# A samples' list on 128 partitions, and half of each gathered row of the second expert table summed on TensorE during the front

## The chip, the cores and the metric

One core of one Trainium2 chip runs the whole program. The metric is device time in microseconds (us); the time of a kernel is the median of its runs. TensorE is PE, its weight loads PEld, VectorE DVE, ScalarE ACT, GpSimd POOL, SyncE SP. SP and POOL issue DMA transfers: SP the plain loads and stores, POOL the gathers.

## The reference, cut to what matters

One decoder layer for 512 prompt tokens and 8 sample tokens, width 1024. After attention, retention and the output projection comes a mixture of 16384 tiny experts, each one row of `peer_u` and one row of `peer_v` (1024 f32 each, 4 KB). Every token picks 16 experts for each of 8 heads:

```
s = jnp.einsum('thcd,hcnd->thcn', q, sub_keys)   # two axes of 128 keys
sv, si = lax.top_k(s, PEER_TOPK)                 # 16 best of each axis
best, pos = lax.top_k(cand, PEER_TOPK)           # 16 best of their 256 sums
g = jax.nn.softmax(best, -1)
u = peer_u[eid]
a = jax.nn.gelu(jnp.einsum('thkd,td->thk', u, xb))
return jnp.einsum('thk,thkd->td', g * a, peer_v[eid])
```

## The kernel before, in words

The program has a **front** (norm, input projection, attention, retention, output projection `out_proj`, second norm `norm2`, and `product_keys`, the choice of the experts) and behind it a **dense loop**. The 512 prompt tokens go through the front in two waves of 256; the 8 samples ride with them.

The first 256 tokens use **gathered** experts. They form two lists of 128 tokens (one on each partition); the 8 samples form a third list, S, of 64 rows: row 8*h+s is head h of sample s. For every head and every one of its 16 experts a *step* fetches one row for each partition with an indirect DMA on POOL's queue (128 rows of 4 KB, 0.524 MB; for S 64 rows) into one of 8 buffers, and does one DVE instruction on it: a *dot* of a `u` row with the token (L940), or a *sum* `y += w*v` of a `v` row over all 1024 columns (L952 for the first, L954). The dots of head h+1 stand ahead of the sums of head h. The generator `work` yields after each step. There are 512 steps of the two lists and 32 of S, 544 in all.

The other 256 tokens, the second wave, use **all** 128 blocks of 128 experts. Block i loads `ut` (512 KB, on SP's queue, 4 buffers), does 8 matmuls of 256 columns (L1058, below called *a block* or *the a's*; they write `paF` while the front runs, `pa` or a spare `y` bank later) and a gelu; then it loads `vt` (512 KB, 4 buffers), multiplies on DVE by `big` (L1173) and does 4 matmuls of 512 columns into the four `y` banks (L1180, *a y*). `big` holds each token's gate for each expert; `scatter` builds it from the top-k lists of wave two, 8 tokens at a time: three one-hot compares on DVE (`oj` L1148, `oi` L1149, and `oi` times the gates, L1153), matmuls into `pg` (L1159), a copy on ACT (L1161). The 32 scatters of the first 64 blocks stand ahead of the first y.

How many steps of `work` go with which part of the front is set by constants. They are emitted 16 at once when wave two begins, then 7 with each piece of its input projection, 5 with each of 8 pieces of `out_proj`, 3 with each of the 8 heads of `product_keys`; SOON of them with the 32 scatters; and RATE minus all those before are paced over the 128 blocks of the dense loop; what is left is emitted behind the last block. While the front runs, `early` also emits 14 of the first 19 a's. Emission sets the data flow, but a scheduler sets the order on each engine.

In `product_keys` of wave two each head takes two `w_pq` loads (1 MB each, `raw`), 16 projection matmuls each of 264 columns (L157), scores (`psco`, L846), and top-k on DVE (from `MAX8`, L258, on); the samples' scores gather in `pss`. Behind the last head the samples' scores are turned (`psr`, L860) and S gets its own top-k (`gS` at L358, `eidS` at L351). Then the gates of wave two are turned (L1116) and the first scatter can begin.

Of the kernel before, what the change touches and what calls it, by code (L numbers as in the profile page):

```python
# [9 lines left out]
F32 = mybir.dt.float32  # L10
F32R = mybir.dt.float32r
BF16 = mybir.dt.bfloat16
I32 = mybir.dt.int32
U32 = mybir.dt.uint32
AF = mybir.ActivationFunctionType
OP = mybir.AluOpType
# [15 lines left out]
GT = 256  # L32
# [11 lines left out]
NG = DT // 8  # L44
STEPS = (16, 7, 5, 3)
BLOCKS = 2
SOON, RATE = 24, 590
AHEAD0 = 14
# [3 lines left out]
def step_kernel(ctx, tc, x_prompt, x_sample, cache_k, cache_v, state_ret, norm1_g, w_in, ret_gn_g,  # L52
# [135 lines left out]

    selb = consts.tile([8, 64], F32, name="selb")
    selT = consts.tile([64, 8], F32, name="selT")  # L190
    iota16 = consts.tile([128, TOPK], BF16, name="iota16")
# [9 lines left out]
    def tables():  # L201
# [28 lines left out]
        nc.vector.tensor_scalar(gnb, gnb, 0.5, None, op0=OP.mult)  # L230
        ii = su.tile([8, 8, 8], I32, name="ii")
        nc.gpsimd.iota(ii, pattern=[[0, 8], [1, 8]], base=0, channel_multiplier=-1)
        nc.vector.tensor_scalar(selb, ii.rearrange("p a b -> p (a b)"), 0.0, None, op0=OP.is_equal)
        pst = ps_tile("tr", "pst")
        nc.tensor.transpose(pst[:64, :8], selb, ident[:8, :8])
        nc.vector.tensor_copy(selT, pst[:64, :8])

# [356 lines left out]
    def samples_attention():  # L594
# [69 lines left out]
        pw = ps_tile("x", "pw")  # L664
        nc.tensor.matmul(pw[:64, :8], selb, snew, start=True, stop=True)
        lnew = sp.tile([64, 1], F32, name="lnew")
# [26 lines left out]
        pw8 = ps_tile("x", "pw8")  # L693
        nc.tensor.matmul(pw8[:8, :8], selT, hsel, start=True, stop=True)
        a8 = sp.tile([8, 512], F32, name="a8", tag="s8")
# [66 lines left out]
    def out_proj(pool, c2, x, xs, ssq):  # L762

        for c, pas in project(w_out2, [c2], range(8)):
            n = WT + (8 if xs is not None else 0)
            cs = slice(c * 128, (c + 1) * 128)
            oT = pool.tile([128, WT + 8], F32, name="oT", bufs=2)
            nc.scalar.activation(oT[:, :n], pas[0][:, :n], AF.Copy)
            pn = ps_tile("tr", "pno")
            for b in range(2):  # L770
                nc.tensor.transpose(pn[:, b * 128:(b + 1) * 128], oT[:, b * 128:(b + 1) * 128], ident)
            nc.vector.tensor_tensor(out=x[:, :, cs], in0=blk(pn[:, :WT]), in1=x[:, :, cs], op=OP.add)
            sq = pool.tile([128, 128], F32, name="osq", bufs=2)
            for b in range(2):
                nc.scalar.activation(sq, x[:, b, cs], AF.Square, accum_out=ssq[:, b, c:c + 1])
            if xs is not None:
                pn2 = ps_tile("x", "pn2o")
                nc.tensor.transpose(pn2[:8, :128], oT[:, WT:], ident)
                nc.vector.tensor_tensor(out=xs[:, cs], in0=pn2[:8, :128], in1=xs[:, cs], op=OP.add)
                nc.scalar.activation(sq[:8], xs[:, cs], AF.Square, accum_out=ssq[:8, 2, c:c + 1])  # L780
            yield

    def norm2(pool, w, x, xs, ssq, hn):
# [24 lines left out]
        if xs is not None:  # L808
            pS = ps_tile("x", "pt2s")
            for k in range(KB):  # L810
# [13 lines left out]
    def product_keys(w, lists, listS, hn):  # L824
# [3 lines left out]
        if w:  # L828
            pss = ps_tile("x", "pss")
        for d in lists:  # L830
# [24 lines left out]
        if w:  # L855
# [63 lines left out]
    def gather(tab, d, h, k, name):  # L919
# [4 lines left out]
        return t  # L924

    def experts(d, rows, hr):
        p, H = d["p"], d["H"]
        y = pe.tile([128, D], F32, name="y", tag="y")[:p]
# [6 lines left out]
        def dots(h):  # L935
            a = pe.tile([128, TOPK], F32, name="a", tag="a", bufs=3)[:p]
            for k in range(TOPK):
                yield
# [3 lines left out]
            w = pe.tile([128, TOPK], F32, name="gw", tag="gw", bufs=3)[:p]  # L942
            nc.scalar.activation(w, a, AF.Gelu_apprx_tanh)
            nc.vector.tensor_tensor(out=w, in0=w, in1=d["g"][:p, h, :], op=OP.mult)
            return w

        def sums(h, w):
            for k in range(TOPK):
                yield
                v = gather(v_tab, d, h, k, "v")  # L950
                if h == 0 and k == 0:
                    nc.vector.tensor_scalar(y, v[:p], w[:, 0:1], None, op0=OP.mult)  # L952
# [39 lines left out]
    def gathered():  # L992
# [3 lines left out]
        store = finish((y[:, 0:512], y[:, 512:]), y, 128, x, yp2[128:GT, :])  # L996
        y64, x = yield from delayed(experts(listS, [hnr[GT:, :]] * 8, slice(512, 520)), 12, store)
        yS = gp.tile([128, D], F32, name="yS", tag="rows")[:8]
# [26 lines left out]
    def run(g, n=1):  # L1025
        for _ in range(n):
            if g is not None:
                next(g, None)

    pools["ap"] = inB.enter_context(tc.tile_pool(name="apB", bufs=2, side="right"))  # L1030

# [266 lines left out]
```

## Time and profile before

| | before |
|---|---|
| median of 3 runs | 1723.51 us (1723.35 to 1728.24) |
| the profiled execution | 1735.22 us, span 1733.3 us |
| PE busy | 1525.3 us, 88% |
| DVE busy | 1209.2 us, 70% |
| ACT busy | 414.0 us, 24% |
| POOL busy | 786.7 us, 45% |
| moved by DMA | 506.88 MB, mean 292 GB/s |
| chain that ended last | PE 65%, DVE 17%, DMA 10%, issue 4% |

The profiled execution is 11.7 us longer than the median of the runs. Its stages, in us from the span's start: wave two's input projection and mixer to about 536 (with gathers from 366 on), `out_proj` and `norm2` to about 598, `product_keys` and the a's to 770, the 32 scatters to 857, the dense loop to about 1635, and the end of it with the samples' list to 1733.

### The profile page before, as it was taken

The page shows a single profiled execution, that of the slowest core. Times are in us where ns is not written, and L with a number is a line of the kernel's source. Part 1 is how long each engine was busy: PE and PEld are TensorE (multiplying, and loading weights), DVE is VectorE, ACT ScalarE, POOL GpSimd, SP SyncE. Part 2 cuts the span into 40 slices and gives each one's busy share as a digit, 9 for nine tenths or more (in the row PEclk, how much of TensorE's full clock was granted, in tenths as well). Part 3 has the DMA queues.
Part 4 walks back from the last instruction along what each step waited for, and adds up shares of the span by engine and source line. Part 5 has one row for each costly group of instructions (what it writes and reads, how often), then busy time and mean ns, then how long its engine had stood idle before and what let it go on. Part 6 is the DMA issues. An engine that isn't in the chain of part 4 may idle for free.

```text
span 1733.3 us, 21787 instructions
## 1 busy us (share of the span) xinstructions
PE 1525.3 (88%) x7544; PEld 1115.3 (64%) x7544; DVE 1209.2 (70%) x2893; ACT 414.0 (24%) x846; POOL 786.7 (45%) x672
## 2 busy tenths in 40 slices
PE   5987679997763698895799999999999999999986
PEld 4976537876652587785566766666766666666632
DVE  5766614688998689999997666666556555555665
ACT  5743623342121211245411121111111000000001
POOL 2155230045567565318366444444445544544551
PEclk9998899998886799995599999999999999999999
DMA  6576574479999899764599999999998999999996
GB/s 195 156 215 206 194 221 129 116 244 349 329 357 355 325 354 355 248 209 143 170 372 388 386 367 327 332 345 350 344 348 315 386 356 368 356 365 363 319 256 182
DMA packets 213326, 506.88 MB, mean 292 GB/s; under 512 B 16424, under 2 KB 103000, under 8 KB 213088
## 3 DMA queue, kind: packets, MB, share of 16 engines
q0 software_dynamic: 82208, 295.80, 47.6%
q1 hardware_dynamic: 131008, 209.68, 36.2%
q8 instruction: 60, 0.98, 0.2%
q14 instruction: 50, 0.41, 0.1%
HBM read 495.56 MB, written 9.86 MB: 292 GB/s over the span
## 4 chain that ended last, share of the span: by engine, by line
PE 65%; DVE 17%; DMA 10%; issue 4%; ACT 1%; POOL 1%; SPq 0%; DVEq 0%; POOLq 0%; ACTq 0%
PE y L1180 23%; PE pa L1058 22%; PE pa L157 8%; DVE u L940 3%; DVE y L954 3%; DMA vt<-in_peer_v 3%; PE pg L1159 3%; DVE oi L1153 2%; DMA raw<-in_w_out 2%; PE paF L1058 1%; DMA raw<-in_w_pq 1%; DVE oj L1148 1%; DMA pq<-sq_d 1%; PE psc L438 1%; PE pa L127 1%
## 5 line engine op out<-in xcount | busy, mean ns | idle before, releaser
L922 POOL DMA_INDIRECT u<-in_peer_u,eidL x256 | 337.6, 1319 | 369.2 <-PE pT L452 113.3
L1180 PE MATMUL y<-vt,ge 128*128 128x512 f32 x1024 | 464.0, 598 | 6.9 <-DMA vt<-in_peer_v 6.7
L922 POOL DMA_INDIRECT v<-in_peer_v,eidL x256 | 322.3, 1259 | 317.9 <-DVE y L954 125.0
L1058 PE MATMUL pa<-hnD,ut 128*128 128x256 f32 x1792 | 407.5, 381 | 0.5 <-ACT ge L1062 0.5
L1058 PEld LDWEIGHTS pa<-hnD,ut 128*128 128x128 f32 x1792 | 338.8, 191 | 76.9 <-issue 35.4
L954 DVE SCALAR_TENSOR_TENSOR y<-v,gw,y 128x1024 f32<-128x1024 f32 (+1 forms) x269 | 346.2, 1287 | 19.5 <-DMA v<-in_peer_v,eidS 12.1
L940 DVE CUSTOM_DVE_ANT_0 u<-u,hq 128x1024 f32<-128x1024 f32 (+1 forms) x272 | 324.2, 1217 | 30.4 <-DMA u<-in_peer_u,eidL 21.0
L1180 PEld LDWEIGHTS y<-vt,ge 128*128 128x128 f32 x1024 | 195.1, 192 | 212.6 <-issue 203.2
L1173 DVE TENSOR_TENSOR ge<-ge,big 128x256 f32<-128x256 f32 x128 | 51.4, 421 | 199.0 <-ACT ge L1062 186.7
L1062 ACT ACTIVATE ge<-pa 128x256 f32<-128x256 f32 x112 | 43.0, 384 | 503.1 <-PE pa L1058 411.9
L157 PE MATMUL pa<-hnD,raw 128*128 128x256 f32 (+1 forms) x512 | 125.1, 398 | 12.1 <-DMA raw<-in_w_pq 12.1
L1159 PEld LDWEIGHTS <-oj 128*128 128x128 bf16 x1536 | 101.0, 167 | 53.3 <-DVE oi L1153 35.1
L157 PEld LDWEIGHTS pa<-hnD,raw 128*128 128x128 f32 x512 | 99.6, 199 | 35.0 <-DMA raw<-in_w_pq 12.9
L157 PE MATMUL pa<-xTB,raw 128*128 128x256 f32 x448 | 105.1, 387 | 2.4 <-ACT pr L547 1.5
L1148 DVE TENSOR_TENSOR oj<-iota,l 128x1024 bf16<-128x1024 bf16 x64 | 44.0, 689 | 74.8 <-PE pg L1159 71.4
L157 PEld LDWEIGHTS pa<-xTB,raw 128*128 128x128 f32 x448 | 84.8, 195 | 14.6 <-ACT pr L547 1.9
L1159 PE MATMUL pg<-oi,oj 128*128 128x64 bf16 x1152 | 76.8, 231 | 15.0 <-DVE oi L1153 14.4
L1161 ACT ACTIVATE big<-pg 128x512 f32<-128x512 f32 x48 | 53.6, 1116 | 145.0 <-PE pg L1159 125.3
L126 PE MATMUL pa<-xT,wh 128*128 128x264 f32 x224 | 70.7, 316 | 8.6 <-ACT xT L119 4.6
L127 PE MATMUL pa<-xT,wh 128*128 128x264 f32 x224 | 68.7, 307 | 0.1
L128 PE MATMUL pa<-xT,wl 128*128 128x264 f32 x224 | 67.7, 302 | 0.6 <-DVE wl L120 0.6
L1153 DVE TENSOR_TENSOR oi<-oi,lx 128x1536 bf16<-128x1536 bf16 x64 | 60.4, 949 | 0.0
(515 smaller groups left out, 1742.9 us busy)
## 6 DMA issues: line engine op xcount, KB each, us to landing
ut<-in_u_turned SPq DMA_DIRECT2D x128, 512.0 KB
vt<-in_peer_v SPq DMA_DIRECT2D x128, 512.0 KB
raw<-in_w_in SPq DMA_DIRECT2D x56, 512.0 KB
raw<-in_w_pq SPq DMA_DIRECT2D x16, 1024.0 KB
raw<-in_w_out SPq DMA_DIRECT2D x8, 1024.0 KB
kv<-in_cache_k_win POOLq DMA_DIRECT2D x24, 256.0 KB
kv<-in_cache_v_win POOLq DMA_DIRECT2D x24, 256.0 KB
u<-in_peer_u,eidL POOLq DMA_INDIRECT x256
```

The lines of the kernel that those rows point to most:

```text
L126: nc.tensor.matmul(out, wh, xh, start=first, stop=False)
L127: nc.tensor.matmul(out, wh, xl, start=False, stop=False)
L128: nc.tensor.matmul(out, wl, xh, start=False, stop=last)
L157: nc.tensor.matmul(pa[:, :n], part[:, k, :], x[0][:, k, :], start=(k == 0), stop=(k == KB - 1))
L922: nc.gpsimd.indirect_dma_start(out=t[:p], out_offset=None, in_=tab, in_offset=bass.IndirectOffsetOnAxis(ap=d["eid"][:p, h, k:k + 1], axis=0))
L940: nc.vector.tensor_tensor_reduce(out=u[:p], in0=u[:p], in1=hn, scale=1.0, scalar=0.0, op0=OP.mult, op1=OP.add, accum_out=a[:, k:k + 1])
L954: nc.vector.scalar_tensor_tensor(y, v[:p], w[:, k:k + 1], y, op0=OP.mult, op1=OP.add)
L1058: nc.tensor.matmul(pa, ut[:, k, :], hnD[:, k, :DT], start=(k == 0), stop=(k == KB - 1))
L1148: nc.vector.tensor_tensor(out=oj, in0=iota128, in1=lJ[:, None, ts].to_broadcast([128, 128, 8]), op=OP.is_equal)
L1153: marks[c] = nc.vector.tensor_tensor(out=oi3, in0=oi[:, None].to_broadcast([128, 3, ne, 64]), in1=lx[:, 1:, None].to_broadcast([128, 3, ne ...
L1159: nc.tensor.matmul(pg_[:, t * ni:(t + 1) * ni], oj[:, :, t], oi3[:, z, :, es], start=(z == 0), stop=(z == 2))
L1180: nc.tensor.matmul(yps[b][q], ge[:, b * 128:(b + 1) * 128], vt[:, q * 512:(q + 1) * 512], start=(i == 0), stop=(i == NKEY - 1))
```

## The change

Part one: S is kept in a second form, `wideS`, on 128 partitions: partition 64*q + 8*h + s holds experts 8*q to 8*q+7 of head h of sample s. So it takes 8 gathers of 128 rows for the dots and 8 for the sums, in place of 16 and 16 of 64 rows. Four small SP transfers (`gW` <- `gS`, `eidW` <- `eidS`, 64x8 each) make it; they stand behind S's top-k. `selb`/`selT`, which sum S's rows for each sample, become 128 wide, and `hq` is loaded in 16 pieces of 8 rows.

Part two: until the front ends, a sum is split. ACT makes `dg` = identity times the weights of the 128 tokens (128x128), PE adds `dg` times the left 512 columns of `v` to a PSUM bank `vsum`, and DVE adds the right 512 columns alone. There are 64 such matmuls (L964 of the new file), and one with a zero `dg` that ends the accumulation; then DVE copies the bank into the left half of `y`. `vsum` holds the PSUM bank "x", so three small users of that bank move to others.

Part three: constants. With 2 in place of 3 steps for each head of `product_keys`, SOON 16 for 24 and RATE 574 for 590, the steps paced over the dense loop stay 402 (590-164-24 and 574-156-16).

```
-STEPS = (16, 7, 5, 3)
+STEPS = (16, 7, 5, 2)
-SOON, RATE = 24, 590
+SOON, RATE = 16, 574
...
-    selb = consts.tile([8, 64], F32, name="selb")
-    selT = consts.tile([64, 8], F32, name="selT")
+    selb = consts.tile([8, 128], F32, name="selb")
+    selT = consts.tile([128, 8], F32, name="selT")
...
-                pn2 = ps_tile("x", "pn2o")
+                pn2 = ps_tile("s", "pn2o")
...
-            pS = ps_tile("x", "pt2s")
+            pS = ps_tile("s", "pt2s")
...
-            pss = ps_tile("x", "pss")
+            pss = ps_tile("o", "pss")
...
             lockstep([tk_finish(qp, listS, 0, 1)])
+            for q in range(2):
+                for nm in ("eid", "g"):
+                    nc.sync.dma_start(wideS[nm][q * 64:(q + 1) * 64, 0, :],
+                                      listS[nm][:64, 0, q * TOPK // 2:(q + 1) * TOPK // 2])
...
+    wideS = {"p": 128, "H": 1, "K": TOPK // 2, "g": pD.tile([128, 1, TOPK // 2], F32, name="gW"),
+             "eid": pD.tile([128, 1, TOPK // 2], I32, name="eidW")}
...
-                if h == 0 and k == 0:
+                if "bank" in half:
+
+                    dg = pe.tile([128, 128], F32, name="dg", tag="dg", bufs=2)
+                    nc.scalar.activation(dg, ident, AF.Copy, scale=w[:, k:k + 1])
+                    nc.tensor.matmul(half["bank"], dg, v[:, :512], start=(h == 0 and k == 0), stop=False)
+                    half["y"] = y
+                    if h == 0 and k == 0:
+                        nc.vector.tensor_scalar(y[:, 512:], v[:p, 512:], w[:, 0:1], None, op0=OP.mult)
+                    else:
+                        nc.vector.scalar_tensor_tensor(y[:, 512:], v[:p, 512:], w[:, k:k + 1], y[:, 512:],
+                                                       op0=OP.mult, op1=OP.add)
+                elif h == 0 and k == 0:
                     nc.vector.tensor_scalar(y, v[:p], w[:, 0:1], None, op0=OP.mult)
                 else:
                     nc.vector.scalar_tensor_tensor(y, v[:p], w[:, k:k + 1], y, op0=OP.mult, op1=OP.add)
...
-        y64, x = yield from delayed(experts(listS, [hnr[GT:, :]] * 8, slice(512, 520)), 12, store)
+        y64, x = yield from delayed(experts(wideS, [hnr[GT:, :]] * 16, slice(512, 520)), 12, store)
...
+    half["bank"] = ps_tile("x", "vsum")
...
     EARLY = step[0]
+
+    dg = pe.tile([128, 128], F32, name="dg", tag="dg", bufs=2)
+    nc.vector.memset(dg, 0.0)
+    nc.tensor.matmul(half["bank"], dg, keysT[:, 0:4, :].rearrange("p a b -> p (a b)"), start=False, stop=True)
+    nc.vector.tensor_copy(half["y"][:, :512], half.pop("bank"))
     front.close()
```

How the change moves the steps, counted in DVE's order: the steps (dots + sums) that stand ahead of five marks.

| mark on DVE | before | after |
|---|---|---|
| last `yo` (L479), end of the mixer | 48 + 30 = 78 | 48 + 21 = 69 |
| `xo` of `norm2` (L797) | 64 + 43 = 107 | 62 + 32 = 94 |
| second `oi` of the scatters (L1153) | 96 + 67 = 163 | 92 + 64 = 156 |
| 32nd of them | 106 + 80 = 186 | 96 + 74 = 170 |
| last `ge` times `big` (L1173) | 502 of 544 | 486 of 528 |

Behind the last mark 42 steps are left in both: 10 sums of list two and 32 of S before, 26 sums and 16 of the wide list after.

On PE, in `product_keys`, at the projections (L157) and scores (L841, L846) of the late heads. Before:

```order
L841 MATMUL pss<-qT,keysT 128x8
L846 MATMUL psco<-keysT,qT 128x128 x3
L157 MATMUL pa<-hnD,raw 128x264 x16
L841 MATMUL pss<-qT,keysT 128x8
L846 MATMUL psco<-keysT,qT 128x128
```

and of the change, at about the same place (L964 is the new matmul, L1079 the a's, which were L1058):

```order
L846 MATMUL psco<-keysT,qT 128x128 x3
L157 MATMUL pa<-hnD,raw 128x264 x3
L964 MATMUL vsum<-v,dg 128x512
L157 MATMUL pa<-hnD,raw 128x264 x2
L964 MATMUL vsum<-v,dg 128x512
L157 MATMUL pa<-hnD,raw 128x264 x3
L841 MATMUL pss<-qT,keysT 128x8
L846 MATMUL psco<-keysT,qT 128x128
L157 MATMUL pa<-hnD,raw 128x264 x3
L964 MATMUL vsum<-v,dg 128x512
L1079 MATMUL paF<-hnD,ut 128x256 x2
L964 MATMUL vsum<-v,dg 128x512
```

The projections of one head, in one piece before, are now cut by `vsum` matmuls, each of which needs its gathered `v` row and its `dg`. Of the 64, 16 stand ahead of `out_proj`, 16 between there and the end of `norm2`, and 32 behind, ahead of the last head's scores.

On PE at the end of `product_keys`, from the last scores to the a's that stand ahead of the first scatter. Before:

```order
L846 MATMUL psco<-keysT,qT 128x128
L1058 MATMUL paF<-hnD,ut 128x256 x8
L841 MATMUL pss<-qT,keysT 128x8
L846 MATMUL psco<-keysT,qT 128x128 x3
L1058 MATMUL paF<-hnD,ut 128x256 x16
L860 MATMUL psr<-ident,sst 64x128 x2
L1058 MATMUL paF<-hnD,ut 128x256 x48
```

and of the change:

```order
L1079 MATMUL paF<-hnD,ut 128x256 x6
L841 MATMUL pss<-qT,keysT 128x8
L846 MATMUL psco<-keysT,qT 128x128 x3
L1079 MATMUL paF<-hnD,ut 128x256 x7
L1115 MATMUL vsum<-keysT,dg 128x512
L860 MATMUL psr<-ident,sst 64x128 x2
L1079 MATMUL pa_6482<-hnD,ut 128x256 x8
```

Before, 8 of the 14 early a's stand behind the last scores, and 9 further a's behind those, ahead of the first `pg`. Now 7 matmuls of one early a stand behind them, and the same 9 further a's: 7.1 blocks have moved ahead of the last scores.

On DVE among the scatters (`oj`, `oi` and the product L1153, now L1174, L1175, L1179; L954 and L974 are sums). Before:

```order
L1149 TENSOR_TENSOR oi<-iotaE,lx 128x512
L1148 TENSOR_TENSOR oj<-iota_6315,l_6319 128x1024
L1153 TENSOR_TENSOR oi_6716<-oi,lx 128x1536
L954 SCALAR_TENSOR_TENSOR y<-v,gw,y 128x1024
L1153 TENSOR_TENSOR oi_6752<-oi,lx 128x1536
L1149 TENSOR_TENSOR oi<-iotaE,lx 128x512
L954 SCALAR_TENSOR_TENSOR y<-v,gw,y 128x1024
L1148 TENSOR_TENSOR oj<-iota_6315,l_6319 128x1024
L1153 TENSOR_TENSOR oi_6788<-oi,lx 128x1536
```

and of the change:

```order
L1174 TENSOR_TENSOR oj<-iota_6491,l_6495 128x1024
L1179 TENSOR_TENSOR oi_6922<-oi,lx 128x1536
L974 SCALAR_TENSOR_TENSOR y<-v,gw,y 128x1024
L1175 TENSOR_TENSOR oi<-iotaE,lx 128x512
L1174 TENSOR_TENSOR oj<-iota_6491,l_6495 128x1024
L1175 TENSOR_TENSOR oi<-iotaE,lx 128x512
L1174 TENSOR_TENSOR oj<-iota_6491,l_6495 128x1024
L1179 TENSOR_TENSOR oi_6958<-oi,lx 128x1536
L1179 TENSOR_TENSOR oi_6997<-oi,lx 128x1536
```

Between the second and the 32nd scatter there were 10 dots and 13 sums; now there are 4 dots and 10 sums.

## Rows read from the trace of the kernel before

**Rows 1.** Windows by stage: engines' busy us, TensorE's granted clock, DMA share, GB/s.

```profile
core 0: us, PE busy (x) PEld busy (x) DVE busy (x) ACT busy (x) POOL busy (x), PEclk, DMA share, GB/s
366.00:536.00 170.00, 117.90 (x571) 96.50 (x571) 151.53 (x454) 38.18 (x74) 105.49 (x85) 0.85 0.97 339
536.00:598.00 62.00, 33.66 (x128) 25.16 (x127) 40.85 (x69) 16.61 (x63) 38.22 (x30) 0.75 0.94 343
598.00:634.00 36.00, 35.64 (x168) 31.04 (x169) 29.89 (x69) 6.67 (x14) 28.47 (x21) 0.88 0.97 358
634.00:701.00 67.00, 62.01 (x303) 53.20 (x303) 66.65 (x261) 13.23 (x32) 34.07 (x31) 0.97 0.96 343
701.00:728.00 27.00, 21.42 (x100) 18.16 (x99) 27.00 (x128) 7.09 (x15) 10.03 (x8) 0.96 0.89 310
728.00:770.00 42.00, 41.38 (x184) 35.64 (x184) 40.90 (x209) 13.40 (x33) 0.24 (x1) 0.94 0.48 155
770.00:857.00 87.00, 53.97 (x794) 50.55 (x793) 86.57 (x134) 45.74 (x63) 48.41 (x25) 0.56 0.54 168
857.00:1635.00 778.00, 778.00 (x3281) 527.68 (x3282) 487.39 (x697) 93.73 (x182) 394.24 (x315) 1.00 0.95 354
1635.00:1733.00 98.00, 79.75 (x173) 32.01 (x171) 65.18 (x90) 11.20 (x22) 35.90 (x35) 0.93 0.87 229
```

**Rows 2.** What PE waited for, 366 to 598: us, times, longest.

```profile
PE py L482 <- DVE yo L479: 34.9, 4, 13.0
PE pa L157 <- DMA raw<-in_w_out: 14.5, 2, 12.6
```

**Rows 3.** What PE waited for, 598 to 701.

```profile
PE pa L157 <- DMA raw<-in_w_pq: 4.9, 2, 3.4
PE pt L804 <- DVE xo L797: 3.6, 1, 3.6
```

**Rows 4.** The chain, dense loop: start, us; x counts matmuls and weight loads.

```profile
892.19 3.45 PE pa L1058 x16
895.64 3.43 PE y L1180 x8
```

**Rows 5.** DVE's timeline: `norm2`, the last head's MAX8, and the first scatters.

```profile
start us, us, engine line op out<-in xcount [idle before <-releaser]
597.56 0.75 DVE L797 TENSOR_SCALAR xo<-xo,rr__5168 128x1024 f32<-128x1024 f32 x1
...
711.12 0.84 DVE L258 MAX8 valL<-sc 128x8 f32<-128x128 f32 x4
...
767.47 1.82 DVE L1153 TENSOR_TENSOR oi<-oi,lx 128x1536 bf16<-128x1536 bf16 x2
```

**Rows 6.** PE's timeline: the last head's scores and what follows.

```profile
700.29 0.92 PE L846 MATMUL psco<-keysT,qT 128*128 128x128 f32 x6
701.04 7.07 PE L1058 MATMUL paF<-hnD,ut 128*128 128x256 f32 x32
```

**Rows 7.** One line's instructions (ns min/median/max): a DVE sum of 512 columns, a 128x128 ACT.

```profile
L1260 DVE SCALAR_TENSOR_TENSOR xb<-xb,rr__11992,gfb x4: 742/743/750, 1727.3 to 1729.3; 128x512 f32<-128x512 f32 x4
...
L775 ACT ACTIVATE osq<-xo x16: 292/294/311, 548.9 to 586.4; 128x128 f32<-128x128 f32 x16
```

**Rows 8.** Where S's gates `gS` end on DVE: ns, start.

```profile
L358 DVE TENSOR_TENSOR gS<-gS,tsm x1: 163/163/163, 750.3 to 750.3; 64x16 f32<-64x16 f32 x1
```

**Rows 9.** DVE by line, 770 to 857: sums and dots among the scatters.

```profile
L954 DVE SCALAR_TENSOR_TENSOR y<-v,gw,y 128x1024 f32<-128x1024 f32 x13 | 16.6, 1278 | 0.0
L940 DVE CUSTOM_DVE_ANT_0 u<-u,hq 128x1024 f32<-128x1024 f32 x13 | 15.7, 1212 | 0.0
```

**Rows 10.** DMA in the dense loop, 1336 to 1635.

```profile
DMA packets 29445, 107.38 MB, mean 359 GB/s; under 512 B 3263, under 2 KB 3263, under 8 KB 29431
```

**Rows 11.** DMA at the end, 1636 to 1714, with the issues of this stretch.

```profile
DMA packets 5845, 20.38 MB, mean 261 GB/s; under 512 B 878, under 2 KB 878, under 8 KB 5842
...
vt<-in_peer_v SPq DMA_DIRECT2D x17, 512.0 KB
...
u<-in_peer_u,eidS POOLq DMA_INDIRECT x16
v<-in_peer_v,eidS POOLq DMA_INDIRECT x16
```

**Rows 12.** DVE by line, 1635 to 1716: the samples' steps, on 64 rows.

```profile
L940 DVE CUSTOM_DVE_ANT_0 u<-u,hq 64x1024 f32<-64x1024 f32 x16 | 19.4, 1215 | 9.3 <-DMA u<-in_peer_u,eidS 9.3
L954 DVE SCALAR_TENSOR_TENSOR y<-v,gw,y 64x1024 f32<-64x1024 f32 x15 | 19.2, 1280 | 12.2 <-DMA v<-in_peer_v,eidS 12.1
```

**Rows 13.** PE's timeline at the end: L1001 sums the samples' rows.

```profile
1712.53 3.67 PE L1180 MATMUL y<-vt,ge 128*128 128x512 f32 x8 [0.39 <-DMA vt<-in_peer_v]
1716.13 1.88 PE L1001 MATMUL pa<-y,selT 64*8 64x512 f32 x4
1717.94 3.70 PE L1180 MATMUL y<-vt,ge 128*128 128x512 f32 x8
```

More of the change, by code (lines that the diff above doesn't have):

```diff
@@ L230, in tables @@
         nc.vector.tensor_scalar(gnb, gnb, 0.5, None, op0=OP.mult)
-        ii = su.tile([8, 8, 8], I32, name="ii")
-        nc.gpsimd.iota(ii, pattern=[[0, 8], [1, 8]], base=0, channel_multiplier=-1)
+        ii = su.tile([8, 16, 8], I32, name="ii")
+        nc.gpsimd.iota(ii, pattern=[[0, 16], [1, 8]], base=0, channel_multiplier=-1)
         nc.vector.tensor_scalar(selb, ii.rearrange("p a b -> p (a b)"), 0.0, None, op0=OP.is_equal)
         pst = ps_tile("tr", "pst")
-        nc.tensor.transpose(pst[:64, :8], selb, ident[:8, :8])
-        nc.vector.tensor_copy(selT, pst[:64, :8])
+        nc.tensor.transpose(pst[:, :8], selb, ident[:8, :8])
+        nc.vector.tensor_copy(selT, pst[:, :8])
     def tk_new(pool, name, p, heads, eid):
@@ L664, in samples_attention @@
         pw = ps_tile("x", "pw")
-        nc.tensor.matmul(pw[:64, :8], selb, snew, start=True, stop=True)
+        nc.tensor.matmul(pw[:64, :8], selb[:, :64], snew, start=True, stop=True)
         lnew = sp.tile([64, 1], F32, name="lnew")
@@ L693, in samples_attention @@
         pw8 = ps_tile("x", "pw8")
-        nc.tensor.matmul(pw8[:8, :8], selT, hsel, start=True, stop=True)
+        nc.tensor.matmul(pw8[:8, :8], selT[:64], hsel, start=True, stop=True)
         a8 = sp.tile([8, 512], F32, name="a8", tag="s8")
@@ L924, in gather @@
         return t
+    half = {}
     def experts(d, rows, hr):
-        p, H = d["p"], d["H"]
+        p, H, K = d["p"], d["H"], d.get("K", TOPK)
         y = pe.tile([128, D], F32, name="y", tag="y")[:p]
@@ L936, in dots @@
             a = pe.tile([128, TOPK], F32, name="a", tag="a", bufs=3)[:p]
-            for k in range(TOPK):
+            for k in range(K):
                 yield
@@ L942, in dots @@
             w = pe.tile([128, TOPK], F32, name="gw", tag="gw", bufs=3)[:p]
-            nc.scalar.activation(w, a, AF.Gelu_apprx_tanh)
-            nc.vector.tensor_tensor(out=w, in0=w, in1=d["g"][:p, h, :], op=OP.mult)
+            nc.scalar.activation(w[:, :K], a[:, :K], AF.Gelu_apprx_tanh)
+            nc.vector.tensor_tensor(out=w[:, :K], in0=w[:, :K], in1=d["g"][:p, h, :], op=OP.mult)
             return w
         def sums(h, w):
-            for k in range(TOPK):
+            for k in range(K):
                 yield
                 v = gather(v_tab, d, h, k, "v")
-                if h == 0 and k == 0:
+                if "bank" in half:
[9 more added lines that the diff above has]
+                elif h == 0 and k == 0:
                     nc.vector.tensor_scalar(y, v[:p], w[:, 0:1], None, op0=OP.mult)
```

## The prediction

> **What bounds the kernel now.** I read the windows by stage first [rows 1]. From 366 to 598 DMA is at 0.97 and 0.94 of its time while PE is busy for 152 of 232 us and DVE for 192: the gathers and the weights set the pace, and PE's waits there are for `yo`, which stands on DVE behind steps, and for weight loads [rows 2]. From 598 to 701 three things are near their limit together: PE 97.7 of 103 us, DVE 66.65 of the last 67, DMA 0.96 to 0.97. From 701 to 770 PE has 62.8 of 69 us, DVE 67.9, and DMA falls to 0.48. Among the scatters DVE is busy for 86.57 of 87 us and PE waits for it. In the dense loop PE is busy for all of 778 us. At the end PE, DVE and DMA all have gaps. So a gain counts in full only where its own resource is the limit: gathers up to 598, PE or DVE up to 770, DVE to 857, PE after that.
>
> A number for "no change": about 0.3%, 5.2 us of 1723.5, is what a measurement of this kernel tells from nothing. The terms below are differences in the profiled execution's own time (1735.22 us, span 1733.3); I take them over to the median, 11.7 us lower, unscaled, since 0.7% of terms of 50 us is nothing.
>
> **The change, part by part.** *Prices.* A gather is 0.524 MB, at the 339 GB/s of [rows 1] 1.54 us of DMA. A `vsum` matmul has the shape of a y's (128x128 by 512 columns): 3.43 us for four in the chain, 0.857 us each; an a is 3.45 us [rows 4]. 32 of the new matmuls are 27.4 us. A sum of 512 columns on DVE is 0.743 us by the same operation of that size [rows 7], against 1.278 of a whole one [rows 9]: 0.535 less. A `dg` on ACT is no more than the 0.3 us of a 128x128 activation [rows 7], and ACT is busy for a fifth of its time there; nothing, unless a matmul waits for its `dg`.
>
> *(1) Up to `norm2`.* By DVE's order 94 steps stand ahead of `norm2`'s `xo` and not 107: 13 gathers fewer, 13 x 1.54 = 20 us if DMA sets the whole stretch, nothing if another does. In this stretch 32 `vsum` matmuls come to PE (27.4 us), which has 80 us free, and DVE is relieved of 17 us besides the 13 steps. DMA's share is 0.94 to 0.97, so I take most of it: **-18** (0 to -20). The half sums by themselves buy nothing here, as neither PE nor DVE is the limit; the shift of steps does.
>
> *(2) From `norm2` to the last scores.* Before, 597.56 [rows 5] to 701.04 [rows 6], 103.5 us. PE gets 32 `vsum` matmuls, 27.4 us, and 7.1 a's that stood behind the scores, 24.5 us: 51.9 more. PE's waits of 8.5 us [rows 3] can take some of it. Bounds +43 and +52, and +35 should a `vsum` cost less than a y's matmul; taken **+45**. DMA agrees: 62 gathers instead of some 30 before the last scores (156 - 94, since every `vsum` stands ahead of them), 15 loads of 1 MB and ten of 0.5 MB are 53 MB, less about 2 MB already under way, at 350 GB/s 146 us, beside the 148.5 of this sum.
>
> *(3) From the last scores to the second `oi`.* Before, 701.04 to 769.3 (767.47 + 1.82) [rows 5], 68.2 us: 10.1 until the last head's MAX8, as DVE was late, then 58.2 with 3 sums and 227 other rows of DVE's order; without the sums (3.8 us) 0.24 us a row. Now 181 rows stand there and no step: 43.3 us. DVE's lateness shrinks too: from `norm2` to that MAX8 its steps are 30 dots and 32 half sums, 60 us, where 32 dots and 21 sums were 66; with 46 rows moved ahead (11 us) it has 119 us of work in 148. I take 4.7 us of delay, 48 in all: **-20.2** (-15 with the old delay, -21). Hidden under it: PE's nine a's (31 us) and the loads `gW`. Those stand on SP's queue ahead of the last two of the nine `ut`, and wait for `gS`; `gS` came 19 us before 769.3 [rows 8], and two a's need 6.9 of it. If the loads take more than 12 us, the first `pg` waits for them. So the scatters begin at -18 + 45 - 20.2 = +6.8.
>
> *(4) The scatters.* DVE sets them. 6 dots and 3 sums fewer stand among them: 6 x 1.212 + 3 x 1.278 [rows 9] = **-11.1** (-9, should DVE wait now and then for PE).
>
> *(5) The dense loop.* PE has no idle time, its work is the same, and 316 steps of whole gathers lie in it in both (186 to 502, 170 to 486): **0**. Were PE to have gaps there, DVE with 487 us of 778 and DMA with 0.95 say that DMA would come next.
>
> *(6) The end.* 42 steps are left behind the last gate product in both, but the 32 on 64 rows were 8.4 MB, and with 10 whole ones 13.6; now 42 whole ones are 22.0 MB. The stretch moved 20.4 MB in 78 us, 261 GB/s [rows 11]; with 8.4 more at the loop's 359 [rows 10] it is 28.8 MB in 80.2 us, +2. DVE's instructions there are as many and as long (1.215 and 1.280 us on 64 rows [rows 12], 1.212 and 1.278 on 128). PE's order has the samples' selector two y's before its end instead of one [rows 13], 3.4 us more if PE waited for the samples; the y just before waited for `vt` and the selector began 0.0 us behind it, so I take none. **+2** (0 to +10).
>
> The 261 GB/s are with 64-row gathers in flight, the 359 with whole ones; the row shows the two rates, not the reason, and DVE waited 21 us for the half gathers. The Trainium skill's page "SBUF — State Buffer" (section "Door 1: The DMA port swizzle (why `[64,N]` ≈ `[32,N]`)") says that partitions 0 to 63 reach 8 of the 16 ports of the memory, so that a transfer to them alone has half the bandwidth. The rates agree with it in kind. By its figure for a large transfer to all 128 partitions, 328 GB/s, the 28.8 MB would be an estimated 88 us, +10 in place of +2.
>
> Sum: -18 + 45 - 20.2 - 11.1 + 0 + 2 = -2.3 us: 1723.5 - 2.3 = **1721**.
>
> **The rivals.**
> *A, the gain of the first stretch stays (faster).* PE's 52 us between `norm2` and the scores shrink: a `vsum` at the 0.592 us that the trace models for a y's matmul instead of 0.857 takes 8.5 off, and the end at nothing 2 more: about -12, 1711. For it: PE has its weights' load beside the matmul. Against: the y's of the same shape never went faster than 0.857 on end.
>
> *B, PE waits for rows (slower).* A `vsum` needs its gathered row, and PE runs in order, so behind a late `v` wait projections, the retention of wave two and then `yo`. In [rows 2] PE never waited for a gather; now it can 64 times, where DMA is at 0.97. If (1) is lost whole, the sum is -2.3 + 18 = +16, 1739. It decides from 8 us lost on. Against: DVE waited for the same rows already, and `yo` stood behind them.
>
> *C, the end keeps its rate (slower).* At 261 GB/s the 28.8 MB are 110 us, +32 instead of +2: 1751. For it: `vt` and gathers share the engines there, and PE waits for `vt`. Against: whole gathers with `vt` and `ut` ran at 359 for 300 us before. By the rule of the Trainium skill named above the half rows were the cause, which would speak against C.
>
> *D, the loads of `gW` block SP (slower).* If the two `ut` behind them come late, first scatter and all after it are later: 10 us, 1731. Against: 12 us of slack in (3).
>
> **How the numbers follow.** The forecast within 5 us of 1721 has 0.37; A 0.34; B 0.15; C 0.06; D 0.08. The forecast lies within 0.3%, except for a small part of it at the lower edge, which about balances what of A falls within; A is faster; B, C and D are slower, though B and D partly occur at sizes that can't be told from none. Faster 0.37, same 0.37, slower 0.26. The range reaches from a full A with the low bound of the end's price (1706) to a full B (1739); it leaves out C and part of the others. The likeliest case's own range is 1716 to 1726.
>
> **What would show it.** (1) `xo` of `norm2` some 18 us earlier, with DMA still above 0.93 ahead of it; PE's waits for `yo` smaller. (2) the last scores 27 us later than 701, PE without idle time since `norm2`. (3) the second `oi` 48 us behind them, at about 776. (4) 76 us of scatters instead of 87. (5) the loop with PE at 100%. (6) the end with over 330 GB/s, and DVE's waits for S's rows gone or short. Wrong it is if PE's list of waits names `v` rows with over 8 us (B), if the stretch behind the loop is over 105 us (C), if the a's ahead of the first `pg` wait for `ut` (D), or if the last scores come by 717 (A).

## The result, and the profile after

The changed kernel is slower: 1739.58 us, median of 7 runs (1733.98 to 1744.4), against 1728.24 for the kernel before beside it (7 runs, 1723.35 to 1732.03). The ratio is 1.0072, 95% interval 1.0047 to 1.0097: some 12 us. Forecast were 1721 and no measurable change.

The profiled execution took 1741.94 us, span 1740.2. The windows by stage of the changed kernel, in the cuts of [rows 1]:

```profile
core 0: us, PE busy (x) PEld busy (x) DVE busy (x) ACT busy (x) POOL busy (x), PEclk, DMA share, GB/s
366.00:536.00 170.00, 145.72 (x671) 112.54 (x670) 136.42 (x455) 50.90 (x106) 99.29 (x81) 0.92 0.96 338
536.00:598.00 62.00, 40.63 (x155) 29.22 (x155) 37.90 (x74) 19.58 (x73) 36.75 (x27) 0.78 0.85 313
598.00:634.00 36.00, 36.00 (x154) 27.18 (x153) 18.32 (x66) 8.49 (x21) 14.68 (x15) 1.00 0.81 271
634.00:701.00 67.00, 61.24 (x256) 46.49 (x254) 56.77 (x251) 16.34 (x39) 35.29 (x32) 0.95 0.94 343
701.00:728.00 27.00, 26.61 (x127) 22.77 (x128) 23.94 (x91) 7.29 (x14) 13.54 (x11) 1.00 0.88 340
728.00:770.00 42.00, 40.41 (x193) 34.81 (x191) 31.29 (x200) 11.95 (x24) 0.00 (x0) 1.00 0.35 108
770.00:857.00 87.00, 55.59 (x773) 52.34 (x772) 84.60 (x156) 47.00 (x73) 39.82 (x16) 0.61 0.43 136
857.00:1635.00 778.00, 776.27 (x3320) 527.51 (x3319) 487.92 (x716) 96.72 (x186) 391.12 (x315) 1.00 0.95 354
```

Read the columns of PE and DVE between 598 and 728. Before, PE was full from 598 to 634 (35.64 of 36 us) and DVE from 634 to 728 (66.65 of 67 and 27.00 of 27). Now PE is full in the first window and in the third (26.61 of 27), and DVE in none: it is busy for 18 of 36 us in the first. DMA, which had 0.96 to 0.97 from 598 to 701, has fallen to 0.81 in the first window: its loads and gathers wait for buffers that PE holds (SP's queue waits 25.4 us for PE there, against 10.2 before; POOL's gathers 8.4 us for `vsum` matmuls).

The marks of the stages, from the timelines of DVE and PE of the changed kernel (they answer to [rows 5, 6]); DVE's `MAX8` of the last head now waits 10.13 us for the scores:

```profile
582.94 0.75 DVE L797 TENSOR_SCALAR xo<-xo,rr__5348 128x1024 f32<-128x1024 f32 x1
```

```profile
739.02 0.91 PE L846 MATMUL psco<-keysT,qT 128*128 128x128 f32 x6
739.78 3.19 PE L1079 MATMUL paF<-hnD,ut 128*128 128x256 f32 x14
...
860.97 8.60 PE L1206 MATMUL y<-vt,ge 128*128 128x512 f32 x16 [1.73 <-DVE ge L1199]
```

```profile
740.61 0.87 DVE L258 MAX8 valL<-sc 128x8 f32<-128x128 f32 x4 [10.13 <-ACT sc L850]
...
782.10 1.82 DVE L1179 TENSOR_TENSOR oi<-oi,lx 128x1536 bf16<-128x1536 bf16 x2
```

`norm2` comes 14.6 us sooner than before, the last scores 39 us later, the second `oi` 14.6 later, the first y 4.2 later. One profile is one execution, and executions differ by some 10 us; so both kernels were profiled a second time (below). The table has, for each profile, the first gathered dot, the stages from mark to mark (first dot, `xo` of `norm2`, start of the last of the last head's scores, end of the second `oi`, start of the first y, start of the last gate product, end of the span), all in us, to about 0.1.

| kernel | first dot at | to `norm2` | to the last scores | to the second `oi` | to the first y | loop | end |
|---|---|---|---|---|---|---|---|
| before | 369.7 | 227.9 | 103.3 | 68.4 | 87.5 | 778.9 | 97.7 |
| before, again | 371.2 | 221.4 | 101.4 | 66.9 | 87.0 | 778.6 | 97.1 |
| the change | 371.1 | 211.8 | 156.8 | 44.2 | 77.1 | 780.6 | 98.6 |
| the change, again | 362.3 | 210.2 | 157.8 | 44.2 | 76.7 | 781.1 | 98.3 |
| list and constants alone | 370.3 | 223.8 | 112.2 | 52.3 | 84.4 | 778.8 | 95.4 |
| half sums alone | 369.3 | 211.7 | 153.6 | 43.6 | 88.1 | 778.5 | 101.8 |
| half sums end ahead of `out_proj` | 373.4 | 201.6 | 115.4 | 67.2 | 75.7 | 780.6 | 98.2 |
| 7 early a's | 366.3 | 217.0 | 129.5 | 43.7 | 85.8 | 779.4 | 94.8 |
| narrow matmuls | 371.7 | 196.8 | 118.4 | 57.0 | 83.4 | 776.3 | 97.8 |
| 7 early a's, no half sums | 369.8 | 222.2 | 101.3 | 53.9 | 87.7 | 779.2 | 94.7 |
| 48 half sums, 10 early a's | 365.4 | 208.8 | 120.7 | 67.2 | 78.2 | 779.6 | 95.7 |
| 4 early a's | 365.6 | 214.3 | 120.4 | 54.1 | 90.3 | 781.3 | 99.3 |
| end ahead of `out_proj`, 7 early a's | 371.2 | 211.7 | 96.3 | 83.8 | 79.1 | 777.2 | 98.7 |

The means of two profiles each give change minus before: -13.7, +55.0, -23.5, -10.4, +2.1, +1.1, in all +10.6 us, against the 12 of the timed runs. The loss lies in one stage, that from `norm2` to the last scores; the stages ahead of it and behind it win most of it back.

### The profile page after: what moved, and what is told of

Its sections match the earlier page's. It is cut to its first block, busy times and chain, and to the rows that moved or that the text cites. A ratio compares the mean times of both kernels' runs of the same rounds, so it can differ in the third digit from the quotient of the medians.

```text
span 1740.2 us, 22103 instructions
## 1 busy us (share of the span) xinstructions
PE 1568.5 (90%) x7674; PEld 1133.5 (65%) x7674; DVE 1158.3 (67%) x2871; ACT 437.2 (25%) x908; POOL 763.9 (44%) x656
## 5 line engine op out<-in xcount | busy, mean ns | idle before, releaser
L929 POOL DMA_INDIRECT u<-in_peer_u,eidL x256 | 329.0, 1285 | 395.7 <-PE pT L452 114.4
L1079 PE MATMUL pa<-hnD,ut 128*128 128x256 f32 x1792 | 407.7, 381 | 1.6 <-issue 1.6
L1079 PEld LDWEIGHTS pa<-hnD,ut 128*128 128x128 f32 x1792 | 338.6, 191 | 77.7 <-issue 36.8
L949 DVE CUSTOM_DVE_ANT_0 u<-u,hq 128x1024 f32<-128x1024 f32 x264 | 315.4, 1221 | 19.9 <-DMA u<-in_peer_u,eidL 19.2
L974 DVE SCALAR_TENSOR_TENSOR y<-v,gw,y 128x1024 f32<-128x1024 f32 x198 | 253.7, 1281 | 22.2 <-DMA v<-in_peer_v,eidL 11.7
L157 PE MATMUL pa<-hnD,raw 128*128 128x256 f32 (+1 forms) x512 | 127.6, 396 | 0.3 <-DMA raw<-in_w_pq 0.3
L157 PEld LDWEIGHTS pa<-hnD,raw 128*128 128x128 f32 x512 | 99.4, 198 | 29.9 <-issue 14.2
L157 PE MATMUL pa<-xTB,raw 128*128 128x256 f32 x448 | 109.0, 394 | 4.5 <-DMA raw<-in_w_in 4.5
L157 PEld LDWEIGHTS pa<-xTB,raw 128*128 128x128 f32 x448 | 86.5, 198 | 21.9 <-issue 8.1
L1174 DVE TENSOR_TENSOR oj<-iota,l 128x1024 bf16<-128x1024 bf16 x64 | 44.0, 688 | 82.6 <-PE pg L1185 75.2
L964 PE MATMUL vsum<-v,dg 128*128 128x512 f32 x128 | 65.8, 610 | 5.9 <-DMA v<-in_peer_v,eidL 5.0
```

Of the source, the lines that this page charges most:

```text
L157: nc.tensor.matmul(pa[:, :n], part[:, k, :], x[0][:, k, :], start=(k == 0), stop=(k == KB - 1))
L929: nc.gpsimd.indirect_dma_start(out=t[:p], out_offset=None, in_=tab, in_offset=bass.IndirectOffsetOnAxis(ap=d["eid"][:p, h, k:k + 1], axis=0))
L949: nc.vector.tensor_tensor_reduce(out=u[:p], in0=u[:p], in1=hn, scale=1.0, scalar=0.0, op0=OP.mult, op1=OP.add, accum_out=a[:, k:k + 1])
L964: nc.tensor.matmul(half["bank"], dg, v[:, :512], start=(h == 0 and k == 0), stop=False)
L974: nc.vector.scalar_tensor_tensor(y, v[:p], w[:, k:k + 1], y, op0=OP.mult, op1=OP.add)
L1079: nc.tensor.matmul(pa, ut[:, k, :], hnD[:, k, :DT], start=(k == 0), stop=(k == KB - 1))
```

## The experiments

Theory 1, formed on these windows: the half sums' matmuls and the a's that now stand among them cost their full time on PE in `product_keys`, because PE had nothing free there; the late scores delay all that follows. Rivals: theory 2, PE's waits for gathered rows in its order, with the slower clock behind one; theory 3, the samples' list or the constants.

**Both kernels once more.**

> The kernel before, unchanged, profiled once more: which of its stages vary from one execution to the next. Its first profile was of an execution of 1735.2 us, above all its seven timed runs (1723.4 to 1732.0). Expected: the first y at 850 to 857 us, the last gate product 778 to 779 us behind it, and the difference to the first profile in the stages ahead of 770 that wait for DMA.

1725.48 us, span 1723.6. The last gate product came 778.6 us behind the first y, as expected; the first y itself came at 847.9, 2 us ahead of the expected 850 to 857. Of the 9.7 us that this execution is shorter than the first, 6.5 lie between the first dot and `norm2`, where DMA is at 0.97 and 0.94 of its time [rows 1], and 1.9 and 1.5 in the two stages behind.

> The changed kernel, unchanged, profiled once more, for what varies between two executions. Expected: from norm2's end to the last scores 152 to 158 us again (157 in its first profile, 101 and 103 in the two of before), the second oi 43 to 46 us behind them, the first y 77 us behind that.

1732.36 us, span 1730.6. The stages from `norm2` on agree with the first profile within about 1 us each; of the 9.6 us between the two executions 8.8 were there at the first dot already (371.1 and 362.3). So the +55 us is no accident of one execution.

**The parts apart.** The list and the constants without the half sums, then the half sums without these:

```
-                if "bank" in half:
...
-                elif h == 0 and k == 0:
+                if h == 0 and k == 0:
```

> The samples' list on 128 partitions and the new constants, without the half sums (each sum is again one DVE instruction of 1024 columns). In its order 155 steps stand ahead of the second oi instead of 163, and 15 among the scatters instead of 23; up to norm2 the order is that of before. Theory 1 (the half sums cost: 32 more matmuls and 7 a's ahead of the last scores on a PE that is full there): none of that is here, so 8 steps less ahead of the scatters and 8 less among them give some -8 to -18 us against before, ratio 0.990 to 0.996. Theory 3 (the loss lies in the samples' list or the constants): +5 us or more, ratio over 1.003.

Ratio 0.9949 (0.9927 to 0.9970), 1718.53 us: faster than before, as theory 1 has it. Theory 3 falls.

```
-STEPS = (16, 7, 5, 2)
+STEPS = (16, 7, 5, 3)
-SOON, RATE = 16, 574
+SOON, RATE = 24, 590
...
-        y64, x = yield from delayed(experts(wideS, [hnr[GT:, :]] * 16, slice(512, 520)), 12, store)
+        y64, x = yield from delayed(experts(listS, [hnr[GT:, :]] * 8, slice(512, 520)), 12, store)
```

> The half sums alone, with the samples' list on 64 partitions and the constants of before (3 steps a head, 24 among the scatters, RATE 590). Theory 1: 68 half sums instead of 64, 34 of them behind norm2, 7 a's moved ahead of the scores as in the change, and 23 steps among the scatters again: the loss of the change without the gain among the scatters, +15 to +25 us against before, ratio 1.009 to 1.014. Theory 3: no slower than before, ratio 0.995 to 1.002.

Ratio 1.0141 (1.0108 to 1.0175), 1748.57 us: the whole loss and more, with 153.6 us from `norm2` to the scores, and 88.1 among the scatters, where 23 steps stand again. The two parts' effects, -0.5% and +1.4%, add up to about the change's +0.7%.

**The half sums ended early.** The zero matmul and the copy of the bank moved ahead of `out_proj`; by the trace 35 half sums are left of 64, and 29 sums are whole again:

```
     inB.close()
+    dg = pe.tile([128, 128], F32, name="dg", tag="dg", bufs=2)
+    nc.vector.memset(dg, 0.0)
+    nc.tensor.matmul(half["bank"], dg, keysT[:, 0:4, :].rearrange("p a b -> p (a b)"), start=False, stop=True)
+    nc.vector.tensor_copy(half["y"][:, :512], half.pop("bank"))
     beside(outer(1, (catB,), hnD, None), 8, STEPS[2])
```

> The change, but the half sums end ahead of out_proj: the bank is copied into y there, and later sums are whole again. 36 vsum matmuls instead of 64, of which 4 stand behind norm2, and 8 a's instead of 13 ahead of the last scores. Theory 1: norm2 ends as early as in the change (583 us against 598), the last scores some 45 us sooner behind it than the change's 157 us, and the whole is 15 to 25 us shorter than the change, -5 to -12 us against before, ratio 0.993 to 0.997. Theory 2 (not PE's work but its waits for gathered rows, and the slow clock behind one, cost: 5 us of wait and some 3 of clock in the change's profile): about 8 us shorter than the change, ratio 1.001 to 1.004.

Ratio 0.9957 (0.9937 to 0.9976), 1717.17 us, within theory 1's interval and below theory 2's. The scores come 115.4 us behind `norm2`, 42 sooner than in the change. But the second `oi` comes 67.2 behind them, and not 44. The windows of this kernel show why:

```profile
575.00:640.00 65.00, 63.98 (x302) 54.19 (x303) 52.52 (x138) 12.05 (x25) 42.69 (x35) 0.93 0.92 325
640.00:700.00 60.00, 54.69 (x256) 46.56 (x255) 60.00 (x262) 14.67 (x32) 27.54 (x25) 0.94 0.89 323
700.00:758.00 58.00, 45.79 (x223) 38.77 (x222) 56.60 (x271) 15.97 (x35) 10.20 (x9) 0.91 0.72 261
```

Once PE is relieved, DVE is the full one (60.00 of 60). From `norm2` to the second `oi` are 182.6 us here, 164.5 in the kernel without half sums: the 13 steps that no longer stand ahead of `norm2` (94 and 107) stand here, at about 1.25 us each on DVE [rows 9]. The half sums' gain up to `norm2` was steps put off, and it is paid behind.

**The a's alone.** One number, and no work added or removed:

```
-AHEAD0 = 14
+AHEAD0 = 7
```

> The change with 7 of the first 19 a's given to product_keys instead of 14: by its order 7 a's stand ahead of the last scores instead of 13, and 12 behind them instead of 10. All other work is the same, and as many half sums stand behind norm2. Theory 1a (what costs is the delay of the last scores, on which the top-k and the scatters wait): 20 us sooner scores, 136 us behind norm2, and 12 to 20 us off the change, -8 to 0 us against before. Theory 1b (what costs is the sum of PE's work ahead of the first scatter, in whichever order): the first pg only 5 to 9 us sooner than the change's 783, +3 to +8 us against before, ratio 1.002 to 1.005.

Ratio 0.9958 (0.9933 to 0.9983), 1718.19 us: theory 1a, 7 us under before and some 20 under the change, with all half sums in place. Theory 1b falls. The scores came 129.5 us behind `norm2` (136 were expected), and the second `oi` 43.7 behind them, as in the change. In this order 97 steps and not 94 stand ahead of `norm2`, which comes 5 to 7 us later behind the first dot. From there to the scores PE is busy for 126.4 us, 23.7 fewer than in the change: 6.1 a's are 21.1 of them, one `vsum` fewer 0.9. It waits 4 us less besides, as the change's wait for a gathered row (shown further down) does not occur in this stage: that is what the expected 136 lacks. The a's put off lie among the scatters now, which take 85.8 us instead of 77. On PE's timeline of this kernel:

```profile
712.12 0.91 PE L846 MATMUL psco<-keysT,qT 128*128 128x128 f32 x6
...
753.41 4.48 PE L1079 MATMUL pa<-hnD,ut 128*128 128x256 f32 x20
757.73 3.04 PE L1185 MATMUL pg<-oi,oj 128*128 128x64 bf16 x48
760.61 5.43 PE L1079 MATMUL pa<-hnD,ut 128*128 128x256 f32 x24
765.87 3.03 PE L1185 MATMUL y<-oi,oj 128*128 128x64 bf16 x48
```

Between the `pg` matmuls, where PE waited for DVE in the kernel before, it now does a's (x20 and x24 are records, two for each matmul): 27 us won ahead of the scores, 9 given back here.

**Narrow matmuls.** The edit is one of width:

```
-                    nc.tensor.matmul(half["bank"], dg, v[:, :512], start=(h == 0 and k == 0), stop=False)
+                    nv = 512 if h == 0 and k == 0 else 128
+                    nc.tensor.matmul(half["bank"][:, :nv], dg, v[:, :nv], start=(h == 0 and k == 0), stop=False)
```

> The change with the vsum matmuls over 128 columns instead of 512, save the first (columns 128 to 511 of the left half of y are left out). Every wait for a gathered row or a dg and every half sum on DVE stays; by its order 33 stand behind norm2 and 9 a's instead of 13 ahead of the last scores. Theory 1 (PE's time for them): 33 matmuls cost about 8 us instead of 28, 4 a's 14 us less: from norm2 to the scores 120 to 137 us (137 if the 48 MB that DMA moved there in the change set it, at 350 GB/s), 12 to 20 us off the change, ratio to before 0.995 to 1.001. Theory 2 (the waits in PE's order for rows): the scores no sooner than the a's alone explain, 143 us, and waits for v of 5 us or more again, ratio 1.002 to 1.006.

Ratio 0.9852 (0.9830 to 0.9873), 1703.18 us: the direction of theory 1, but 36 us off the change and not 12 to 20. `norm2` to the scores took 118.4 us, as theory 1 had it; besides that, 88 steps stand ahead of `norm2` in its order instead of 94, and it came 13 to 15 us sooner. So the 36 us bound PE's part from above. In the stage itself the account comes out: PE is busy for 115.5 us there, 34.6 fewer than in the change, and 32 matmuls of a quarter of the columns (20.6) and 4.1 a's (14.2) are 34.8. (The kernel leaves out columns of the left half, so it is a measurement and not a kernel to keep.) The expectation's 137 us for DMA did not bind because other bytes fell in the stage, 42 MB and not 48; at 354 GB/s and 0.97 of its time DMA was near its limit here.

**A control, and three tries for more.** The control has the smaller number of early a's without half sums:

> A control for the run with 7 a's in product_keys: the same constant, but without half sums (the samples' list on 128 partitions and the new constants alone). By its order 5 a's stand ahead of the last scores instead of 8. Theory 1a (the a's cost only where PE, filled by the half sums, sets when the last scores come): DVE sets this stretch here (busy for 59.7 of 60 us and 43.1 of 45 in the run without half sums), so nothing changes against that run, ratio to before 0.992 to 0.998. Theory 4 (7 is simply the better constant and the half sums had no part in it): some 15 to 20 us less than without it, ratio 0.983 to 0.987.

Ratio 0.9927 (0.9900 to 0.9955), 1710.60 us, the best of the kernels that do all of the work. It lies where theory 1a put it, near the lower edge; its interval overlaps that of the same kernel with 14 a's (0.9927 to 0.9970), so a further gain is not shown. On the change the same number is worth 1.1%, and theory 4's 15 to 20 us are excluded. But "nothing changes" does not fit the profile: the scores came 101.3 us behind `norm2` and not 112.2, and PE was busy for 93.7 us there and not 104.5, the 10.3 us of three a's. So the a's cost in this stage without half sums as well; 3.3 us of it are given back among the scatters. The two profiles are one execution each.

With 48 half sums (the bank is closed in `sums`, at the 49th) and `AHEAD0 = 10`:

> The change, but the half sums end with the 48th sum, and 10 of the first 19 a's are given to product_keys. By its order 17 half sums stand behind norm2 and 6 a's ahead of the last scores. PE then has 14 us more than before ahead of the scores, and DVE is relieved of 9 us in the same stretch. Theory 1: the scores 112 to 120 us behind norm2, the second oi 50 to 55 behind them, and the whole 2 to 8 us under the run whose half sums end ahead of out_proj; ratio to before 0.990 to 0.995. If instead any half sum behind norm2 is a loss: 3 us or more over that run, ratio over 0.997.

Ratio 0.9981 (0.9958 to 1.0003), 1719.93 us: a miss. The scores came 120.7 us behind `norm2`, near the forecast, but the second `oi` 67.2 behind them and not 50 to 55; DVE is busy for all of 640 to 700 here too (60.00 us; PE 57.15). Against the run that ends the half sums ahead of `out_proj` (0.9937 to 0.9976) the intervals overlap.

With `AHEAD0 = 4` on the change:

> The change with 4 of the first 19 a's given to product_keys, instead of 14 or 7: 4 stand ahead of the last scores by its order, and all 33 half sums still lie behind norm2. Theory 1a: the last scores another 8 to 10 us sooner behind norm2 than with 7 (129.5 us there) as far as DMA lets them, the scatters then slower by some of it, as more a's lie among them; 0 to 6 us under that run, ratio to before 0.992 to 0.997. Theory 1b (the sum of PE's work counts): the same as with 7 to within 2 us.

Ratio 0.9981 (0.9957 to 1.0005), 1721.78 us: also a miss, no better than with 7. The scores did come 9 us sooner (120.4), but the second `oi` 10 later behind them and the first y 4.5 later behind that: DVE is busy for all of 640 to 700 (PE for 58.97), and the a's put off fill the scatters.

With both repairs, end ahead of `out_proj` and `AHEAD0 = 7`:

> The change with both repairs: half sums end ahead of out_proj, and 7 of the first 19 a's are given to product_keys (by its order 3 half sums behind norm2, 2 a's ahead of the last scores, 21 behind them). If DVE sets the stretch from norm2 to the second oi once PE is relieved, it stays at 175 to 183 us (182.7 with 14 a's) and the whole within 4 us of that run, ratio to before 0.993 to 0.998. If the early a's still cost there, 8 us or more less, ratio under 0.992; then the half sums' gain up to norm2 and the moved a's add up, and this beats the run without half sums and with 7 a's (0.9927).

Ratio 0.9952 (0.9931 to 0.9973), 1717.45 us; 180.1 us from `norm2` to the second `oi`, where 175 to 183 were expected if DVE sets it. The scores come after 96.3 us and then wait for DVE for 83.8.

## Why the prediction was wrong

It named the stages and the signs of the terms rightly, but its sum, -2.3, was +10.6 in the profiles and +12 in the runs.

**(1) Up to `norm2`: -18 forecast, -13.7 measured.** The mechanism held up to 536: DMA was at 0.96 of its time and 338 GB/s, and PE's wait for `yo` fell from 34.9 us [rows 2] to 2.2. Behind that, up to `norm2`, DMA was at 0.83 and 305 GB/s (0.93 and 342 before), and PE waited 13.3 us for `norm2`'s `xo` on ACT (8.5 before); so it was two thirds of the 13 gathers' 20 us and not most of it. Nor are these steps saved. The prediction took them as covered by PE's longer stage behind `norm2`; the run with the half sums ended ahead of `out_proj` shows that they cost there, on DVE, as soon as PE is relieved.

**(2) `norm2` to the last scores: +45 forecast, +55 measured. This is the step that failed.** The price of a `vsum` matmul was right. PE's timeline of the changed kernel:

```profile
616.61 1.02 PE L964 MATMUL vsum<-v,dg 128*128 128x512 f32 x2
617.47 0.59 PE L1079 MATMUL paF<-hnD,ut 128*128 128x256 f32 x2
617.90 1.02 PE L964 MATMUL vsum<-v,dg 128*128 128x512 f32 x2
```

From 616.61 to 617.47 are 0.86 us, as the 0.857 of [rows 4] said. (One of them makes two records.) So 32 of them are 27.4 us, and 7.1 a's 24.5, as forecast: 51.9. Wrong was the 7 us taken off, on the ground that PE's waits of [rows 3] would take some of it in. In this stage PE was busy for 150.1 and 150.2 us in the two profiles of the change and for 97.7 and 97.6 in the two of before: +52.5. It was idle for 6.9 and 7.8 us, and before for 5.8 and 4.0: +2.5, where the prediction had some -7. Together they are the +55. The old waits shrank (from 8.5 us to 1.4), and others came in their place. PE's waits from 583 to 741:

```profile
PE vsum L964 <- DMA v<-in_peer_v,eidL: 5.0, 1, 5.0
PE pt L804 <- DVE xo L797: 1.4, 1, 1.4
PE paF L1079 <- issue: 0.8, 1, 0.8
PE vsum L964 <- ACT dg L963: 0.4, 1, 0.4
```

The second profile has the wait for a `v` row too, 5.2 us. It costs more than itself. PE's timeline around it, and the windows there (the number behind the engines' columns is the granted clock):

```profile
645.78 2.39 PE L157 MATMUL pa<-hnD,raw 128*128 128x264 f32 x10
653.16 2.08 PE L964 MATMUL vsum<-v,dg 128*128 128x512 f32 x2 [4.99 <-DMA v<-in_peer_v,eidL]
655.03 6.21 PE L157 MATMUL pa<-hnD,raw 128*128 128x264 f32 x18
661.08 1.02 PE L964 MATMUL vsum<-v,dg 128*128 128x512 f32 x2
```

```profile
645.00:660.00 15.00, 10.01 (x31) 7.15 (x30) 13.15 (x47) 1.28 (x4) 11.33 (x9) 0.77 0.99 385
660.00:701.00 41.00, 40.23 (x173) 29.95 (x171) 34.13 (x176) 13.29 (x31) 15.21 (x16) 1.00 0.91 326
```

Behind 5 us without work the same matmul takes 2.08 us instead of 1.02, and 9 projection matmuls (18 records) 6.2 us instead of about 4: the granted clock of 645 to 660 is 0.77, that behind it 1.00, and twice the time is the lower of the two levels, 1.2 GHz for 2.4. The wait and its slow stretch are some 8 us: rival B in small, at one place and not 64 times. It is not the main cause, as the busy and idle times above show. The run with 7 a's doesn't settle this by itself: it has the same 64 matmuls and is 20 us shorter, but this wait is gone from its stage too.

The other half of the failure is what the term rests on. The 24.5 us of a's ahead of the scores were read out of the order and costed rightly, but taken as if the change had to bring them. They are independent work, put in front of the scores that the scatters wait for, on an engine with little room (busy for 97.65 of 103 us before [rows 1]). Before, they stood behind the scores, in time that DVE's top-k covered. The experiment that puts some 6 of them back behind the scores, with which the wait leaves this stage too, is worth 20 us, more than the whole loss.

DMA's sum beside this term, 53 MB and 146 us, was miscounted, and its agreement with 148.5 was chance. A head takes one `w_pq` load of 1 MB and not two, as the kernel's description has it, so 6 and not 15 were issued in this stage; and before, 51 gathers and not some 30 were issued there. The change moved 47.6 MB in it at 304 GB/s and 0.84 of DMA's time: DMA did not set its length.

**(3) Scores to the second `oi`: -20.2 forecast, -23.5 measured.** DVE was no longer late, as argued, and even less so: it waited for the scores, 10.13 us ahead of the last head's `MAX8`. The loads `gW` did not hold up the first `pg`: PE waited there for `oi` (5.3 us), not for `ut`. Rival D did not occur.

**(4) The scatters: -11.1 forecast, -10.4 measured.** In the windows from 784 to 861 DVE has 5 dots and 12 sums where [rows 9] had 13 and 13. (By this count 91 dots and not 92 stand ahead of the second `oi`.)

**(5) The loop: 0 forecast, +2.1.** PE is busy for all but 1.7 us of its window, and no run explains the difference; the loops of all thirteen profiles lie between 776.3 and 781.3.

**(6) The end: +2 forecast, +1.1.** The DMA of the end, 1642 to 1712, in the changed kernel:

```profile
DMA packets 7429, 27.08 MB, mean 387 GB/s; under 512 B 825, under 2 KB 825, under 8 KB 7425
```

With gathers of 128 rows in flight the end moves at 387 GB/s, where it had 261 with gathers of 64 rows [rows 11]; it moves 27.1 MB in 70 us, and before 20.4 in 78; rival C is refuted. The rate goes with the list and not with the half sums: with the list alone the end moves at 386 GB/s (1630 to 1700), with the half sums alone, on 64 rows, at 251 (1645 to 1724). The Trainium skill, in "SBUF — State Buffer" (section "Door 1: The DMA port swizzle (why `[64,N]` ≈ `[32,N]`)"), has a transfer to partitions 0 to 63 reach half the ports; by that rule the rate should rise with the wide list, and the trace agrees, 261 to 387. (The 328 GB/s that the prediction takes from the Trainium skill stands there for a transfer of 1 MiB, and this stretch moved more.) A gather of 64 rows also holds half the bytes, and no run separates that from the ports. The nearness of +1.1 to +2 is in part luck: DMA was faster than the 359 GB/s of the sum, and PE waited 4.7 and 6.2 us for the samples' sums in the two profiles of the change, a wait that the prediction took as none. In the two kernels with the list and no half sums PE had no such wait, and the end is 95.4 and 94.7 us, against 97.1 and 97.7 before.

Rival A did not occur: no two `vsum` matmuls on end came closer than 0.857. The sum missed by 12.9 us: 10 of them are (2), 4.3 are (1), 2.1 the loop, and (3) was 3.3 better. The chance for slower (0.26) rested on mishaps, while the plain sum of PE's work, 52 us at its own upper bound, already gave +5 with the rest as forecast.

## What to carry to other kernels

Work moved to an engine that is busy for 95% of a stage can cost its whole time there: here 51.9 us of work cost 55. Don't credit the receiving engine's waits without a row that shows them filled; here others took their place. When an order shows independent work sliding ahead of the operation that a later stage waits for, ask first whether it can be put back behind it: here that was worth 20 us of the change for one constant, though going on from 7 to 4 won nothing more. And count where put-off steps land: a stage that ends sooner because a step left it has gained only if the stage that receives it has room.

## What the runs showed of the hardware

Behind one wait of 5 us for a gather, PE's matmuls took twice their time for some 6 us; the granted clock is 0.77 over the 15 us around it and 1.00 behind. With gathers to 128 partitions beside plain 512 KB loads the end moved 387 GB/s, and with gathers to 64 partitions beside the same loads 261. One f32 matmul of 128x128 by 512 columns took 0.857 us on end. Two executions of one kernel differed by up to 10 us in where they were at the first gather or at `norm2`, while every stage behind agreed within 2 us: profiles are best compared from mark to mark.
